# The eight column-tiled output matmuls of a state-space channel group, issued as one run led by the last state

## The chip, the cores and the metric

The kernel runs on one core of a Trainium2 chip. Its time is the device time of one execution in microseconds (us); of several executions the median is taken. The engines are named as in the profile: PE is TensorE (matmuls), PEld its weight loads, DVE is VectorE, ACT is ScalarE, POOL is GpSimd, SP is SyncE, which here only issues DMAs. Each engine works through its own queue in the order in which its instructions were put there.

## The reference, cut to what matters

One layer of a decoder trunk with 256 positions and 4096 channels, everything in float32. A normalised input is multiplied by one combined projection, whose columns feed three mixers (pooling, stick-breaking attention and a state-space mixer); the gated mixer outputs go through one output projection and a final norm. The change lies in the state-space mixer, of which this is the core:

```python
bu = jnp.einsum('blgc,gpc->blgp', ug.astype(jnp.complex64), b_bar)
a = jnp.broadcast_to(lam_bar, bu.shape)
...
_, states = lax.associative_scan(combine, (a, bu), axis=1)
y = jnp.einsum('blgp,gcp->blgc', states, c_mat).real.reshape(bsz, L, D_SSM)
y = y + d_skip.astype(jnp.float32) * uf
h = jax.nn.gelu(y)
```

There are 64 groups of 16 channels with 64 complex states each. The change concerns the second product: the real part of the states times the complex output matrix, that is, real part times real part minus imaginary times imaginary.

## The kernel before

**The main stream.** All large products are one stream of 528 weight blocks of 256 rows by 512 columns (the list `subs`; the projection, the gated linear unit of the state-space mixer, and the output projection one after the other). A block is loaded by SP (`load`, L175), split by ACT into a high part (`hi`, L120 through `hi_lo`, L210) and by DVE into the remainder (`lo`, L212), and then multiplied in `mm_tok`: for each half of the positions and each of the two row tiles three matmuls, high by high (L317), high by low (L324) and low by high (L325), into the PSUM tile `pm`. Loads run four blocks ahead and splits two blocks ahead of the matmuls; the split parts go round in a ring of four buffers. In the output stage some blocks go through `mm_seven` (L284) with seven products in place of eight.

**Side work.** The mixers are generators that yield after each small step. They wait in two queues, `side_q` and `ssm_q`; after each block `pump` takes some steps from them, for the state-space mixer 1.5 a block from block 30 on. This fixes the program order. What each engine does in which order is then planned by the framework from that order, the dependencies and a timeline simulation (`schedule_with_timeline_sim=True`, L1167); only SP's order is that of the program. A dependency of the kind NoSync that is added by hand with `tc.add_manual_dep` holds two instructions of the plan in order and adds no semaphore.

**The state-space mixer.** `ssm` works through eight channel groups `ct` of 128 channels, that is, eight of the reference's groups in each. For each group it makes `cf`, the output matrix with its scale, then four states `ss[0]` to `ss[3]`, each for two of the reference's groups (128 partitions, two components of 256 positions). Each state takes a PE product (`ps_bu`, L650), the rotation by tables (L658 to L662), two scans (L665), and the rotation back (L667, L668); component 0 is made at L670 and component 1, last of all, at L671. Four buffers (`s`) hold the states.

**The output matmuls.** When the fourth state is appended, L674 takes one of two PSUM banks shared by the small products (`ps`), and eight matmuls follow at L677: for each component `c` and each state `j`, the 128 rows of `cf[:, j, c, :]` with 32 columns as weights, the 256 positions of `ss[j][:, c, :]` as moving data, into the partitions 32j to 32j + 31 of `ps_y`. A matmul with 32 columns uses a quarter of the PE array, a column tile; the four values of `j` use four different ones. Component 0 starts the sum and component 1 closes it. Since the operands are float32, each such matmul is shown as two instructions in the trace. The matmuls of `c` = 0 need `ss[j][:, 0, :]` alone, so they may leave before the later states are there.

Behind them, DVE adds the skip term (`y`, L682, shown as L117) and reads `ps_y`; ACT and DVE make the GELU, and its product goes back into `uT(ct)` (L687), which the gated linear unit reads much later. The next group's `cf` and states may only overwrite the old ones when the eight matmuls are done.

Of the kernel before, what the change touches and what calls it, by code (L numbers as in the profile page):

```python
# [21 lines left out]
L = 256  # L22
# [55 lines left out]
def body(tc, a, out, ctx):  # L78
    nc = tc.nc
    V, S, T, G = nc.vector, nc.scalar, nc.tensor, nc.gpsimd  # L80
# [512 lines left out]
    def ssm(sp, wait_u):  # L593
# [11 lines left out]
        for ct in range(8):  # L605
# [5 lines left out]
            cf = sp.tile([P, 4, 2, 32], F32, tag="cf", bufs=1, name="cf")  # L611
# [6 lines left out]
            ss = []  # L618
            for half in range(2):
# [3 lines left out]
                for m in range(4, 8):  # L623
                    n = 1 << m
                    for j in range(2):
                        c, sn = (pw[:, m, x, 4 * ct + 2 * half + j:4 * ct + 2 * half + j + 1] for x in range(2))
# [19 lines left out]
                for j in range(2):  # L646
                    pr = 4 * ct + 2 * half + j
                    ps = pk.tile([P, 2, L], F32, tag="ps", bufs=2, name="ps_bu")
# [23 lines left out]
                    ss.append(s)  # L672
                    yield
            ps = pk.tile([P, 512], F32, tag="ps", bufs=2, name="ps_y")  # L674
            for c in range(2):
                for j in range(4):
                    T.matmul(ps[32 * j:32 * j + 32, 0:L], cf[:, j, c, :], ss[j][:, c, :], start=c == 0, stop=c == 1, skip_group_check=True)  # L677
            yield
            y = sp.tile([P, L], F32, tag="yg", bufs=1, name="y")
            z = sp.tile([P, L], F32, tag="zg", bufs=1, name="z")  # L680
# [139 lines left out]
    ep = op = None  # L820
    apool = None
    ssm_q.append(ssm(sp, lambda ct: ct < u_done[0]))
    glu_sums = cp.tile([P, 2, 2], F32, name="glu_sums")
    out_sums = cp.tile([P, 2, 4], F32, name="out_sums")
# [152 lines left out]
    for i, (ui, at, h, s) in enumerate(subs):  # L977
        kind, c, nk = units[ui]
# [8 lines left out]
        if at == 0 and h == 0:  # L987
# [4 lines left out]
            else:  # L992
                ps = [pm.tile([P, NU], F32, tag="c%d" % t, bufs=2, name="pm") for t in range(2)]
# [16 lines left out]
        if seven(i):  # L1010
            if h == 0:
# [4 lines left out]
                j = SEVENS[c].index(s)  # L1016
# [37 lines left out]
    for t in range(2):  # L1054
        for h, at, wide, dst in ((0, 0, NU, out_sums[:, t, 3:4]), (1, 0, half, sums[:, t, 0:1]), (1, half, half, sums[:, t, 1:2])):
# [9 lines left out]
            if h == 0:  # L1065
                ss = cp.tile([P, 1], F32, name="ss_out%d" % t)
# [111 lines left out]
```

## Time and profile before

| | |
|---|---|
| median of three runs | 1518.77 us (1517.45 to 1519.06) |
| the profiled execution, its own time | 1519.82 us |
| the profiled execution, its span (first to last instruction) | 1518.0 us |
| mean granted TensorE clock | 0.998 of full speed |
| instructions | 19823 |
| bytes read and written | 371.28 MB and 48.76 MB |
| instructions of line 677 on PE | 128, from 185.1 to 780.4 us |

A busy time in the profile is the sum over an engine's instructions where overlapping ones count once. Ends of matmuls are modelled, so a matmul's shown duration is longer than the distance between two starts; distances between starts show the rate. A row of the timeline merges neighbouring instructions of one line (the number behind x). A window's row gives, for each engine, the busy time and the number of instructions in it. The chain of work follows the end of the execution back from instruction to instruction, each to what released it or to the one before it on its engine. "issue" is time in which an engine waited for nothing that the profile shows.

### The profile page before, as it was taken

How to read it: one execution, taken by the hardware profiler on the slowest of the kernel's cores; microseconds unless marked ns; L12 is line 12 of the kernel's file. 1: busy time of each engine (PE TensorE's matmuls, PEld its weight loads, DVE VectorE, ACT ScalarE, POOL GpSimd, SP SyncE). 2: the span in 40 equal slices, each digit the busy share in tenths (PEclk: the TensorE clock that was granted, in tenths of full speed). 3: DMA queues.
4: the chain of work that ended last, by engine and by line, in shares of the span. 5: the costliest groups of instructions: out<-in, count | busy, mean ns of one | idle time of the engine just before them, and what ended most of it. 6: DMA issues, size and time to landing. Idle time of an engine off the chain costs nothing.

```text
span 1518.0 us, 19823 instructions
## 1 busy us (share of the span) xinstructions
PE 1501.9 (99%) x6848; PEld 1232.7 (81%) x6848; DVE 1223.9 (81%) x1876; ACT 878.0 (58%) x1165; POOL 15.2 (1%) x31
## 2 busy tenths in 40 slices
PE   9999999999999999999999999999999999999996
PEld 7888888787878788888888888888888778888885
DVE  7479978898989898999875555576657898989897
ACT  7655455665655555545655544565546776757574
POOL 0000000000000000000000000000000000000000
PEclk9999999999999999999999999999999999999999
DMA  9766556576788886888678788689977989889895
GB/s 359 297 227 211 192 169 209 189 229 235 269 286 302 297 289 233 309 302 302 231 272 299 266 309 284 244 301 348 339 244 255 355 332 349 311 328 322 311 367 211
DMA packets 129508, 424.50 MB, mean 280 GB/s; under 512 B 15616, under 2 KB 21504, under 8 KB 129408
## 3 DMA queue, kind: packets, MB, share of 16 engines
q1 hardware_dynamic: 115504, 398.17, 74.1%
q0 software_dynamic: 3760, 14.16, 2.4%
q10 hardware_dynamic: 10144, 10.92, 2.4%
q8 instruction: 53, 0.87, 0.2%
q14 instruction: 47, 0.39, 0.1%
HBM read 371.28 MB, written 48.76 MB: 277 GB/s over the span
## 4 chain that ended last, share of the span: by engine, by line
PE 92%; DMA 3%; DVE 3%; issue 1%; ACT 0%; SPq 0%; DVEq 0%; ACTq 0%
PE pm L317 26%; PE pm L325 26%; PE pm L324 26%; PE p L284 6%; PE pm L284 5%; DMA w<-in_ws 2%; DVE lo L212 1%; PE ps_y L677 1%; PE ps_c L771 1%; PE ps_bu L650 1%; DMA yk<-kept 1%; PE ps_p L459 0%; PE ps_t L375 0%; PE ps_z L702 0%; DVE ts L108 0%
## 5 line engine op out<-in xcount | busy, mean ns | idle before, releaser
L212 DVE TENSOR_TENSOR lo<-w,hi 128x1024 fp32r<-128x1024 f32 (+1 forms) x531 | 619.7, 1174 | 233.2 <-ACT hi L120 231.6
L120 ACT ACTIVATE hi<-w 128x1024 fp32r<-128x1024 f32 (+1 forms) x531 | 539.1, 1020 | 461.8 <-PE pm L325 350.6
L324 PE MATMUL pm<-lo,xhl 128*128 128x512 f32 x1714 | 669.2, 391 | 0.7 <-DVE lo L212 0.7
L325 PE MATMUL pm<-hi,xhl 128*128 128x512 f32 x1714 | 669.0, 391 | 0.0
L317 PE MATMUL pm<-hi,xhl 128*128 128x512 f32 x1714 | 661.1, 391 | 1.2 <-ACT xhl L120 0.6
L317 PEld LDWEIGHTS pm<-hi,xhl 128*128 128x128 f32 x1714 | 322.2, 188 | 69.7 <-issue 2.1
L325 PEld LDWEIGHTS pm<-hi,xhl 128*128 128x128 f32 x1714 | 322.2, 188 | 68.2 <-issue 2.9
L324 PEld LDWEIGHTS pm<-lo,xhl 128*128 128x128 f32 x1714 | 322.4, 188 | 67.8 <-DVE lo L212 1.6
L120 ACT ACTIVATE hi<-t 128x1024 fp32r<-128x1024 f32 x84 | 86.2, 1052 | 38.0 <-DVE t L108 20.8
L212 DVE TENSOR_TENSOR lo<-t,hi 128x1024 fp32r<-128x1024 f32 x84 | 100.9, 1221 | 4.1 <-ACT hi L120 3.6
L284 PE MATMUL pm<-hi,xhl 128*128 128x512 f32 x168 | 65.5, 390 | 0.0
L284 PE MATMUL p<-hi,xhl 128*128 128x512 f32 x168 | 65.2, 391 | 0.0
L284 PE MATMUL p<-hi,y 128*128 128x512 f32 x168 | 64.1, 389 | 0.0
L117 DVE SCALAR_TENSOR_TENSOR et<-et,pw,tr 128x16 f32<-128x16 f32 (+3 forms) x256 | 55.8, 276 | 3.0 <-ACT tr L120 2.7
L120 ACT ACTIVATE tr<-et,pw 128x32 f32<-128x32 f32 (+3 forms) x128 | 44.9, 384 | 17.9 <-DVE et L117 8.3
L108 DVE TENSOR_TENSOR pre<-pre 128x512 f32<-128x512 f32 x68 | 46.7, 687 | 0.9
L665 DVE TENSOR_TENSOR_SCAN tb<-rho,ta 128x256 f32<-128x256 f32 x64 | 40.6, 676 | 0.2
L284 PEld LDWEIGHTS p<-hi,xhl 128*128 128x128 f32 x168 | 31.5, 188 | 7.4 <-ACT hi L120 1.0
L284 PEld LDWEIGHTS p<-hi,y 128*128 128x128 f32 x168 | 31.5, 188 | 6.5
L284 PEld LDWEIGHTS pm<-hi,xhl 128*128 128x128 f32 x168 | 31.5, 188 | 6.5
L284 PE MATMUL pm<-hi,y 128*128 128x512 f32 x84 | 32.8, 390 | 1.1 <-ACT hi L120 1.1
L284 PE MATMUL p<-lo,xhl 128*128 128x512 f32 x84 | 32.8, 391 | 0.1
(248 smaller groups left out, 1174.8 us busy)
## 6 DMA issues: line engine op xcount, KB each, us to landing
w<-in_ws SPq DMA_DIRECT2D x493, 512.0 KB, 4.9
pre<-in_ws SPq DMA_DIRECT2D x68, 512.0 KB, 7.0
sums<-pre SPq DMA_DIRECT2D x68, 512.0 KB, 5.5
t<-sums SPq DMA_DIRECT2D x68, 512.0 KB, 7.4
w<-in_ws SPq DMA_DIRECT2D x36, 256.0 KB, 6.9
xsq<-in_xr SPq DMA_DIRECT2D x8, 512.0 KB, 6.5
o<-in_xr SPq DMA_DIRECT2D x8, 512.0 KB, 8.3
xt<-in_xT SPq DMA_DIRECT2D x15, 256.0 KB, 6.1
```

The lines of the kernel that those rows point to most:

```text
L108: V.tensor_tensor(o, x, y, op)
L117: V.scalar_tensor_tensor(o, x, s, y, op0, op1)
L120: return S.activation(o, x, f, **kw)
L212: state["split"] = V.tensor_tensor(dst_lo, src, dst_hi.bitcast(F32), ALU.subtract).ins.name
L284: T.matmul(o, stat[:, p, :], pair[q][:, n], start=start and k == 0, stop=stop and k == 2, skip_group_check=True)
L317: made = T.matmul(o, stat[:, slot, 0, sl], hi[:, n], start=begin, stop=False, skip_group_check=True)
L324: T.matmul(o, stat[:, slot, 0, sl], lo[:, n], start=False, stop=False, skip_group_check=True)
L325: made = T.matmul(o, stat[:, slot, 1, sl], hi[:, n], start=False, stop=end, skip_group_check=True)
L650: T.matmul(ps[:, c, :], b3r[:, j, c, :], u3r[:, j, :], start=c == 0, stop=True, skip_group_check=True)
L665: V.tensor_tensor_scan(tb[:, c, :], rho[:, pr:pr + 1].broadcast_to([P, L]), ta[:, c, :], 0.0, ALU.mult, ALU.add)
L677: T.matmul(ps[32 * j:32 * j + 32, 0:L], cf[:, j, c, :], ss[j][:, c, :], start=c == 0, stop=c == 1, skip_group_check=True)
L771: T.transpose(ps[:, (c * 2 + t) * P:(c * 2 + t + 1) * P], z[:, t, (h * 2 + c) * P:(h * 2 + c + 1) * P], ident)
```

## The change

The order of the eight matmuls is turned round: component 1 comes first and now starts the sum, component 0 closes it; within a component the state order is 3, 0, 1, 2. The first matmul therefore reads component 1 of state 3. Each of the other seven is given a NoSync dependency on this first one, so that none of them can stand ahead of it in PE's order. Operands, sizes and the number of instructions stay as they are.

```diff
             ps = pk.tile([P, 512], F32, tag="ps", bufs=2, name="ps_y")
-            for c in range(2):
-                for j in range(4):
-                    T.matmul(ps[32 * j:32 * j + 32, 0:L], cf[:, j, c, :], ss[j][:, c, :], start=c == 0, stop=c == 1, skip_group_check=True)
+            first = None
+            for c in (1, 0):
+                for j in (3, 0, 1, 2):
+                    made = T.matmul(ps[32 * j:32 * j + 32, 0:L], cf[:, j, c, :], ss[j][:, c, :], start=c == 1, stop=c == 0, skip_group_check=True)
+                    if first is None:
+                        first = made.ins.name
+                    else:
+                        tc.add_manual_dep(
+                            made.ins, first,
+                            mybir.DependencyInfo(mybir.DependencyClass.NoSync, mybir.DependencyReason.DATA),
+                            reason="all in one run",
+                        )
             yield
```

## The prediction

> **What bounds the kernel now.** I read the page's engine totals first, then the chain that ended last, then the waits of TensorE. From the page:
>
> ```profile
> PE 1501.9 (99%) x6848; PEld 1232.7 (81%) x6848; DVE 1223.9 (81%) x1876; ACT 878.0 (58%) x1165; POOL 15.2 (1%) x31
> ...
> PE 92%; DMA 3%; DVE 3%; issue 1%; ACT 0%; SPq 0%; DVEq 0%; ACTq 0%
> PE pm L317 26%; PE pm L325 26%; PE pm L324 26%; PE p L284 6%; PE pm L284 5%; DMA w<-in_ws 2%; DVE lo L212 1%; PE ps_y L677 1%; PE ps_c L771 1%; PE ps_bu L650 1%; DMA yk<-kept 1%; PE ps_p L459 0%; PE ps_t L375 0%; PE ps_z L702 0%; DVE ts L108 0%
> ```
>
> TensorE (PE) is busy for 99% of the span and carries 92% of the chain. Matmuls of the weight stream (L317, L324, L325) make up most of it, and the matmuls of this change (ps_y, L677) stand on the same chain with about 1%. So the question is how much PE time the eight output products take, and how much of that is the price of being issued in pieces.
>
> A busy PE can hide slow issue, so I measure in starts. The PE timeline around channel group 0 (start, length of the merged row, line, count):
>
> ```profile
> 182.75 0.39 PE L325 MATMUL pm<-hi,xhl 128*128 128x512 f32 x1
> ...
> 184.79 0.39 PE L325 MATMUL pm<-hi,xhl 128*128 128x512 f32 x1
> 185.11 0.63 PE L677 MATMUL ps_y<-s,cf 128*32 128x256 f32 x6
> 185.68 0.50 PE L317 MATMUL pm<-hi,xhl 128*128 128x512 f32 x1
> 186.01 0.39 PE L324 MATMUL pm<-lo,xhl 128*128 128x512 f32 x1
> ...
> 187.63 0.39 PE L325 MATMUL pm<-hi,xhl 128*128 128x512 f32 x1
> 187.95 1.05 PE L677 MATMUL ps_y<-s,cf 128*32 128x256 f32 x10
> 188.93 0.50 PE L317 MATMUL pm<-hi,xhl 128*128 128x512 f32 x1
> 189.26 0.39 PE L324 MATMUL pm<-lo,xhl 128*128 128x512 f32 x1
> ```
>
> The first two rows are nine stream matmuls apart: (184.79 - 182.75) / 9 = 0.227 us a start. Around the ps_y run of six, two stream starts that would be 0.454 us apart (184.79 to the second stream matmul after the run, 186.01) are 1.22 us apart: the run costs 0.77 us. The run of ten costs 187.63 to 189.26 less 0.454, 1.18 us. Each column matmul shows as two instructions, so these are three matmuls (states 0, 1, 2 of component 0) and five (the rest).
>
> Two groups are cut three times, as the timeline around group 2 shows:
>
> ```profile
> 336.41 0.39 PE L317 MATMUL pm<-hi,xhl 128*128 128x512 f32 x1
> 336.73 0.62 PE L677 MATMUL ps_y<-s,cf 128*32 128x256 f32 x4
> 337.29 0.50 PE L324 MATMUL pm<-lo,xhl 128*128 128x512 f32 x1
> 337.62 0.39 PE L325 MATMUL pm<-hi,xhl 128*128 128x512 f32 x1
> ```
>
> ```profile
> 343.55 0.39 PE L324 MATMUL pm<-lo,xhl 128*128 128x512 f32 x1
> 343.87 0.62 PE L677 MATMUL ps_y<-s,cf 128*32 128x256 f32 x2
> 344.42 0.50 PE L325 MATMUL pm<-hi,xhl 128*128 128x512 f32 x1
> 344.75 0.39 PE L317 MATMUL pm<-hi,xhl 128*128 128x512 f32 x1
> ```
>
> In the same way the run of four costs 1.21 - 0.454 = 0.76 us and the run of two 1.20 - 0.454 = 0.75 us. What is to be seen: two, four or six instructions last 0.62 to 0.63 us and cost the same, 0.75 to 0.77 us. Products that go to different column tiles lie beside each other; only the two instructions of one tile follow each other. The run of ten is longer because column tile 3 has two matmuls in it, four instructions deep: (1.05 - 0.62) / 2 = 0.215 us a level. So a run's price is a fixed part for entering and leaving the narrow tiles, 0.75 - 2 x 0.215 = 0.32 us, plus 0.215 us for each level of its deepest tile.
>
> How many runs there are comes from the windows of line 677, one window for each group (PE busy, then the count):
>
> ```profile
> 180.00:190.00 10.00, 1.68 (x16) 0.53 (x16) 1.00 0.67 211
> ...
> 334.00:358.00 24.00, 2.29 (x16) 0.66 (x16) 1.00 0.67 217
> ...
> sum 139.00, PE 14.69 PEld 4.48; mean PE 1.84 PEld 0.56
> ```
>
> 1.68 is one run of 0.63 and one of 1.05; 2.29 is two of 0.62 and one of 1.05. The sum 14.69 over eight windows is six of the first kind and two of the second (6 x 1.68 + 2 x 2.29 = 14.66). So today there are 6 x 2 + 2 x 3 = 18 runs.
>
> **The change part by part.** *Removed:* ten of the 18 runs. *Added:* six instructions (in the two groups with three runs, three matmuls from two places) to the last run of each group, which then holds all 16. The tile order 3, 0, 1, 2 repeated twice puts four instructions on every column tile, so the deepest tile stays at four levels: 0.32 + 4 x 0.215 = 1.18 us, and I add 0.02 us for the wider lower levels: 1.20 us. No trace shows 16 in one run. The bounds: not below the 1.18 us of the run of ten, which is as deep; at most six more levels in single file, 1.18 + 6 x 0.215 = 2.47 us. I take 1.20 because runs of two, four and six already differ by 0.02 at most.
>
> Saved in a two-run group: 0.77 + 1.18 - 1.20 = 0.75 us; in a three-run group 0.76 + 0.75 + 1.18 - 1.20 = 1.49 us. Sum: 6 x 0.75 + 2 x 1.49 = **7.5 us**. At the upper bound it would be 6 x (1.95 - 2.47) + 2 x (2.69 - 2.47) = -2.7 us, a loss.
>
> One rule of the Trainium skill speaks against the packed figure. The window of 0.2 us at the head of the run of ten shows, for this line, PE and then weight loads (PEld):
>
> ```profile
> 187.90:188.10 0.20, 0.15 (x4) 0.15 (x8) 1.00 1.10 328
> ```
>
> Eight weight loads start within 0.15 us while four matmuls are in flight, so loads for narrow tiles lie beside matmuls and beside each other. The page "TensorE: Matmul & The Clock Gate", section Part 3: Packing small matmuls — row/col tiling, says that a weight load overlaps with matmuls in flight only where the row group differs; all column tiles here use the same 128 rows, so by it none would. Here the trace speaks against it.
>
> *Moved:* the whole product now waits for the state made last, component 1 of state 3, which leads. Today the first run leaves before that. An added wait on PE holds up everything behind it, here the stream matmuls, and behind them ScalarE, which waits for PE to free the split buffers, and VectorE's y. What does the wait cost? From the VectorE timeline for groups 0 and 5 (s is the state, both components merged), and from the PE timeline for group 5:
>
> ```profile
> 183.66 0.75 DVE L108 TENSOR_TENSOR s<-ta,tb 128x256 f32<-128x256 f32 x2
> ...
> 603.08 0.76 DVE L108 TENSOR_TENSOR s<-ta,tb 128x256 f32<-128x256 f32 x2
> ```
>
> ```profile
> 607.15 1.05 PE L677 MATMUL ps_y<-s,cf 128*32 128x256 f32 x10
> ```
>
> State 3 is complete at 184.41 and 603.84; the run of ten starts at 187.95 (above) and 607.15. So both components lie ready 3.5 and 3.3 us before the run leaves. Component 1 is made one VectorE step (about 0.4 us) after component 0, which released that run in the plan; the new lead moves later by about that, and the margin stays. I take nothing for the wait, covered by these 3 us. Without the cover each microsecond of standing costs 8 us over the groups. Below nothing it cannot go: the run cannot leave before the state is there.
>
> The run of ten also tells whether all 16 will stay together: there, too, one matmul is released by the newest state and four that were ready follow it, and it stands uncut in the groups quoted and, by the windows (one more cut would add a run of 0.62), in all eight. No DMA is issued or moved, and no VectorE or ScalarE instruction is added. The first matmul of each accumulation now is component 1 instead of 0; that costs nothing.
>
> **Does the end follow?** PE time saved between 185 and 781 us reaches the end only if nothing else limits the later work:
>
> ```profile
> 450.00:800.00 350.00, 350.00 (x1649) 286.65 (x1648) 312.33 (x530) 189.76 (x263) 1.07 (x2) 1.00 0.82 283
> 1300.00:1400.00 100.00, 100.00 (x442) 82.79 (x442) 92.83 (x100) 68.56 (x79) 0.68 (x1) 1.00 0.89 320
> ```
>
> PE has no idle time in either stretch; VectorE is next, at 312.33 / 350 = 89% and 93%. Shortening the first stretch by about 1% takes VectorE to about 90%: it becomes tighter, not the bound. From the table of waits:
>
> ```profile
> ACT hi L120 <- PE pm L325: 355.3, 266, 2.9
> ```
>
> The splitting of weights, and with it VectorE and the loads, waits for PE for 355.3 us in total. These move forward with PE, so I carry the whole 7.5 us to the end. The profiled execution took 1519.82 us, its span 1518.0; it would become 1512.3 with a span of 1510.5. The median of the runs before is 1518.77, 1.05 below the profiled execution, so I predict a median of 1518.77 - 7.5 = **1511.3 us**.
>
> **The rivals.** *Part of the gain given back by a new plan.* The instruction order is planned over the whole program, so a change at 185 us can move splits, loads and side work after it. The table of PE's waits has these of the stream's own (line, what it waited for: total, times, longest):
>
> ```profile
> PE pm L284 <- ACT hi L120: 1.1, 1, 1.1
> PE pm L317 <- DVE gl L108: 0.7, 1, 0.7
> PE pm L324 <- DVE lo L212: 0.7, 1, 0.7
> PE pm L317 <- ACT xhl L120: 0.6, 1, 0.6
> PE pm L317 <- DVE ss_out L1067: 0.5, 1, 0.5
> ```
>
> These are 3.6 us. If a new order brings as many again, the time is 1511.3 + 3.6 = 1514.9. VectorE's 93% in the output stage speaks for it; that the table has only one more, ahead of the first matmuls of all, speaks against it.
>
> *Swallowed in the output stage.* The chain that ended last leaves PE in that stage (start, length):
>
> ```profile
> 1428.29 0.24 PE pm L325
> ...
> 1428.56 0.97 ACT hi L120
> ...
> 1431.95 6.71 DMA w<-in_ws
> ```
>
> If loads and VectorE bound that stage by themselves, the saved time would turn into stalls there: 1518.8. Against it: the chain enters this piece from a split (ACT hi, 1428.56) that starts as a matmul ends, so the piece moves with PE.
>
> *The run does not stay whole.* If the planner sends the lead alone and the other 14 later, each group has a run of two (0.75) and one of 14 (at most 1.20): nothing saved in six groups, 2 x 0.74 = 1.5 us in two: 1517.3. Against it stands the uncut run of ten.
>
> *Weight loads between the levels.* Levels three and four hold one load each today and four then. If three more loads of 0.109 us had to stand in each, that is 2 x 3 x 0.109 = 0.65 us a group, 5.2 us: 1516.5.
>
> ```profile
> L677 PEld LDWEIGHTS ps_y<-s,cf x128: 106/109/110, 185.1 to 780.2; 128*32 128x32 f32 x128
> ```
>
> That is how the rule of that page of the Trainium skill would come out. The eight loads in 0.15 us speak against it.
>
> *Slower: PE stands at the lead.* The waits of VectorE for this product today (total, times, longest):
>
> ```profile
> DVE y L117 <- PE ps_y L677: 6.6, 7, 1.8
> ```
>
> Once the lead is at the head of PE's queue, the stream behind it cannot pass. It decides from 7.5 / 8 = 0.94 us of standing a group. The plan's clock and the chip's differ: VectorE today waits up to 1.8 us for ps_y, PE today has 3.3 us to spare. Were this turned round and PE waited 1.8 us in every group, 8 x 1.8 = 14.4 us would be added: 1511.3 + 14.4 = 1525.7. For it: only the planner's clock keeps the margin. Against it: the margin is above 3 us in the groups read, and the lead moves later by only one VectorE step.
>
> **How the numbers follow.** Forecast 0.66; part given back 0.14; swallowed 0.06; not whole 0.04; weight loads 0.03; slower 0.07 (in it 0.02 for a run in single file, 1518.8 + 2.7 = 1521.5). A measurement of this kernel tells about 0.2%, 3.0 us, from no change: faster is below 1515.7. Of the part given back I count 0.09 as faster and 0.05 as the same. Faster: 0.66 + 0.09 = 0.75; same: 0.05 + 0.06 + 0.04 + 0.03 = 0.18; slower 0.07. The range goes from 1508.8 (a new plan that also removes 2.5 of the 3.6 us of stalls) to 1517.0, which leaves out the swallowed, the cut and the slower cases, 0.17.
>
> **What would show it.** Right: eight ps_y runs of 16, each lasting about 1.07 us and costing about 1.20 us between stream matmuls; line 677's weight loads idle before them eight times, not 18; no PE wait on a state. Wrong: runs cut by stream matmuls; a run above 1.3 us; an idle PE ahead of ps_y released by VectorE; or new PE stalls after 800 us that add up to the missing time.

## The result, and the profile after

The changed kernel takes **1510.47 us** (median of four, 1510.05 to 1511.52) against 1518.91 us of the kernel before (median of four, the three above and one more): a ratio of 0.9945, 95% interval 0.9932 to 0.9957, 8.4 us less. The forecast was 1511.3 us. The profiled execution took 1510.62 us with a span of 1508.8 us; before it was 1518.0 us.

From the page of the changed kernel, engine totals and the chain that ended last:

```profile
PE 1492.9 (99%) x6848; PEld 1232.6 (82%) x6848; DVE 1222.3 (81%) x1876; ACT 878.5 (58%) x1165; POOL 15.2 (1%) x31
...
PE 94%; DMA 2%; DVE 2%; issue 1%; ACT 0%; SPq 0%; DVEq 0%; ACTq 0%
```

PE's busy time fell by 9.0 us with the same 6848 matmuls, and the span by 9.2; the other engines did the same work as before. The bound is the same, PE at 99%, with less to do. Line 677 is now line 678. Its windows, one for each channel group as before (PE busy, count; weight loads, count), the first and the last of eight:

```profile
180.00:190.00 10.00, 1.07 (x16) 0.42 (x16) 1.00 0.67 197
...
765.00:782.00 17.00, 1.07 (x16) 0.42 (x16) 1.00 0.89 308
sum 149.00, PE 8.56 PEld 3.34; mean PE 1.07 PEld 0.42
```

The sum 8.56 is eight times 1.07: each product is one run, where before the eight windows held 14.69. What such a run costs is read from the PE timeline of group 0:

```profile
188.44 0.39 PE L325 MATMUL pm<-hi,xhl 128*128 128x512 f32 x1
188.76 1.07 PE L678 MATMUL ps_y<-s,cf 128*32 128x256 f32 x16
189.76 0.50 PE L317 MATMUL pm<-hi,xhl 128*128 128x512 f32 x1
190.10 0.40 PE L324 MATMUL pm<-lo,xhl 128*128 128x512 f32 x1
```

The stream starts around it lie 190.10 - 188.44 = 1.66 us apart; less two undisturbed steps of 0.227 us the run costs 1.21 us. Sixteen instructions cost 0.03 us more than the ten of before (1.18). This is the only run of the eight that stands alone. Six others have a pair of `ps_bu` matmuls directly behind them, and the last has four of `ps_c` beside it. In group 2 the run and its pair cost 1.45 us together (359.24 - 357.34 - 0.454); the 20 pairs that stand alone cost 0.25 us each on average, so 1.20 us is left for the run.

The wait that the change adds, in group 5, which had the smallest margin of the groups read before (VectorE, then PE timeline):

```profile
599.45 0.76 DVE L108 TENSOR_TENSOR s<-ta,tb 128x256 f32<-128x256 f32 x2
```

```profile
603.09 1.07 PE L678 MATMUL ps_y<-s,cf 128*32 128x256 f32 x16
```

State 3 is complete at 600.21 and the run leaves at 603.09: 2.9 us of cover are left of 3.3. Read in the same way in all eight groups, the cover is 2.9 to 4.5 us; ahead of the last run of each group before it was 3.3 to 5.0 us. The table of PE's waits has no row for ps_y at all:

```profile
PE ps_i L137 <- DVE zeros L134: 1.2, 1, 1.2
PE pm L317 <- ACT hi L120: 1.2, 1, 1.2
PE pm L317 <- ACT xhl L120: 0.9, 1, 0.9
PE pm L317 <- DVE gl L108: 0.7, 1, 0.7
PE pm L317 <- DVE ss_out L1076: 0.5, 1, 0.5
PE pm L284 <- ACT hi L120: 0.3, 1, 0.3
PE pm L324 <- DVE lo L212: 0.2, 1, 0.2
```

Behind the first row, which lies ahead of the stream, these are 3.8 us; before they were 3.6. So the saving was not paid back in new stalls. The line's weight loads, too, idle before them eight times, where before it was 18 times, once for each run.

### The profile page after: what moved, and what is told of

Its sections match the earlier page's. It is cut to its first block, busy times and chain, and to the rows that moved or that the text cites. A ratio compares the mean times of both kernels' runs of the same rounds, so it can differ in the third digit from the quotient of the medians.

```text
span 1508.8 us, 19821 instructions
## 1 busy us (share of the span) xinstructions
PE 1492.9 (99%) x6848; PEld 1232.6 (82%) x6848; DVE 1222.3 (81%) x1876; ACT 878.5 (58%) x1165; POOL 15.2 (1%) x31
## 4 chain that ended last, share of the span: by engine, by line
PE 94%; DMA 2%; DVE 2%; issue 1%; ACT 0%; SPq 0%; DVEq 0%; ACTq 0%
PE pm L317 26%; PE pm L325 26%; PE pm L324 26%; PE p L284 7%; PE pm L284 5%; DMA w<-in_ws 2%; DVE lo L212 1%; PE ps_c L780 1%; PE ps_bu L650 1%; PE ps_y L678 1%; PE ps_p L459 0%; PE ps_z L711 0%; PE ps_t L375 0%; DVE ts L108 0%; DMA prm<-in_prm 0%
## 5 line engine op out<-in xcount | busy, mean ns | idle before, releaser
L324 PE MATMUL pm<-lo,xhl 128*128 128x512 f32 x1714 | 668.4, 390 | 0.2 <-DVE lo L212 0.2
L317 PE MATMUL pm<-hi,xhl 128*128 128x512 f32 x1714 | 660.5, 391 | 2.6 <-ACT hi L120 1.2
L317 PEld LDWEIGHTS pm<-hi,xhl 128*128 128x128 f32 x1714 | 322.1, 188 | 69.5 <-ACT xhl L120 1.8
L284 PE MATMUL pm<-lo,xhl 128*128 128x512 f32 x84 | 32.7, 389 | 0.0
```

What stands on the lines that cost most here:

```text
L284: T.matmul(o, stat[:, p, :], pair[q][:, n], start=start and k == 0, stop=stop and k == 2, skip_group_check=True)
L317: made = T.matmul(o, stat[:, slot, 0, sl], hi[:, n], start=begin, stop=False, skip_group_check=True)
L324: T.matmul(o, stat[:, slot, 0, sl], lo[:, n], start=False, stop=False, skip_group_check=True)
```

## The experiments

### The order without the dependencies

The order of the change is kept and the added dependencies are dropped.

```diff
-                    if first is None:
-                        first = made.ins.name
-                    else:
-                        tc.add_manual_dep(
...
-                            reason="all in one run",
-                        )
```

Expected:

> The changed order of the eight matmuls without the added dependencies. Theory (the lead by the state made last holds the run together, the dependency adds nothing): eight runs of 16 instructions, 1510.5 us. Rival (the dependency holds the run together): 18 runs as before, 1518.9 us.

Measured: 1509.78 us, ratio to before 0.9945 (0.9928 to 0.9961). The windows of line 678 sum to the same as with the dependencies:

```profile
sum 149.00, PE 8.56 PEld 3.34; mean PE 1.07 PEld 0.42
```

Eight whole runs, so the dependencies add nothing; on every engine the instructions stand in the same order as in the changed kernel. What holds the seven others back is the plan itself. In all the kernels here the lengths of the runs fit a plan that keeps the eight matmuls in the order of the program. The kernel before shows it too: at 185.11 six instructions left, those of component 0 of states 0 to 2, though component 1 of these states lay ready as well; in the kernel that goes state by state, below, twelve leave at that place. So whichever matmul stands first in the program holds back the other seven. That the planner does this because all eight write one PSUM tile is likely, but no run tests it.

### Component 1 first, led by the state made first

The kernel before, with only the components exchanged.

```diff
-            for c in range(2):
+            for c in (1, 0):
                 for j in range(4):
-                    T.matmul(..., start=c == 0, stop=c == 1, skip_group_check=True)
+                    T.matmul(..., start=c == 1, stop=c == 0, skip_group_check=True)
```

Expected:

> The kernel before with component 1 first and the states in their old order 0, 1, 2, 3, without dependencies: the lead is the state made first. Theory (only a lead by the state made last keeps the run whole): 18 runs as before, 1518.9 us. Rival (turning the components round is what brings the gain): 1510.5 us.

Measured: 1518.45 us, ratio 1.0001 (0.9992 to 1.0011). The windows of line 677 in this kernel, the first and the last of eight:

```profile
180.00:190.00 10.00, 1.68 (x16) 0.53 (x16) 1.00 0.72 209
...
765.00:782.00 17.00, 1.68 (x16) 0.53 (x16) 1.00 0.79 276
sum 152.00, PE 14.69 PEld 4.49; mean PE 1.84 PEld 0.56
```

The busy sum is that of the kernel before, and so is the time. Turning the components round brings nothing by itself.

### Component 0 first, led by the state made last

The changed kernel, with the components put back.

```diff
-            for c in (1, 0):
+            for c in (0, 1):
                 for j in (3, 0, 1, 2):
-                    made = T.matmul(..., start=c == 1, stop=c == 0, skip_group_check=True)
+                    made = T.matmul(..., start=c == 0, stop=c == 1, skip_group_check=True)
```

Expected:

> The changed kernel with component 0 first again, still led by state 3 and with the dependencies. The lead is one VectorE step older than in the changed kernel. The planned order differs in some places from the changed kernel's. Theory (the lead by the last state is all that matters, and the wait for its second component is covered): eight runs of 16, PE never idle ahead of them, 1510.5 us, within 2 us. Rival (the wait for component 1 costs or gains something, or the new plan and not the runs brought the gain): more than 2 us away from 1510.5.

Measured: 1510.47 us, ratio 0.9949 (0.9936 to 0.9961). Again eight whole runs:

```profile
sum 149.00, PE 8.57 PEld 3.34; mean PE 1.07 PEld 0.42
```

Which component of state 3 leads makes no difference that can be measured. With the run before this separates the parts of the change: the lead by the last state carries all of it. It also speaks against a lucky plan: this kernel's order differs from the changed kernel's in places on PE, VectorE and ScalarE, and its time is the same.

### Both matmuls of a tile next to each other

The changed kernel, with the loops exchanged; the run stays whole, the order inside is 3, 3, 0, 0, 1, 1, 2, 2.

```diff
-            for c in (1, 0):
-                for j in (3, 0, 1, 2):
+            for j in (3, 0, 1, 2):
+                for c in (1, 0):
```

Expected:

> The changed kernel with the two loops exchanged, so that the two matmuls of a column tile stand next to each other (3, 3, 0, 0, 1, 1, 2, 2); the run stays whole. Theory A (a run lasts as long as its deepest column tile, whatever the order inside): a run costs 1.20 us as in the changed kernel, 1510.5 us. Theory B (matmuls start strictly in the order of the queue, so a tile waits until the second matmul of the tile before it has started): the four tiles follow one another, three of them add two to three levels of 0.215 us each, 1.3 to 1.9 us a run, 10 to 16 us in all: 1521 to 1526 us.

Measured: 1510.24 us, ratio 0.9949 (0.9934 to 0.9964). The PE timeline has the run of group 0:

```profile
187.76 1.09 PE L678 MATMUL ps_y<-s,cf 128*32 128x256 f32 x16
```

It is 0.02 us longer, not 1.3 to 1.9. The window of 0.2 us at its head holds these instructions of the line on PE:

```profile
187.75:187.95 0.20, 0.19 (x4) 1.00 1.06 318
```

Four instructions are in flight within 0.2 us, less than the 0.215 us of one level, although the program's first four instructions (two matmuls) all belong to tile 3. So tiles do not queue behind one another: theory A, the depth of the deepest tile, holds, and theory B falls. The page "TensorE: Matmul & The Clock Gate" of the Trainium skill says in its section Part 3: Packing small matmuls — row/col tiling that matmuls start and end strictly in program order; with the program's order here that would have been theory B. Whether PE starts them out of order or the two instructions of each matmul are already put in another order in the queue, the trace, which knows starts, does not tell.

### State by state, in the order in which the states are made

The kernel before, with the loops exchanged. This cuts the product more often.

```diff
-            for c in range(2):
-                for j in range(4):
+            for j in range(4):
+                for c in (0, 1):
```

Expected:

> The kernel before with the two loops exchanged, so that both matmuls of a state stand together and the states follow in the order in which they are made. In the planned order the product is then cut into 22 runs in place of 18: eight of one matmul, six of two, two of four, six of six. Theory (0.32 us for a run and 0.215 us for each level of its deepest tile, all of it on the path): 8 x 0.75 + 6 x 1.18 + 2 x 1.18 + 6 x 1.20 = 22.6 us against 17.1 us before: 1518.9 + 5.5 = 1524.4 us. Rival (the price of the cuts is hidden, and the gain came from the new plan): within 2 us of 1518.9.

Measured: 1524.20 us, ratio 1.0040 (1.0025 to 1.0055), 5.9 us above the 1518.28 us of the kernel before beside it. The PE timeline of group 0, whose product is now cut into three:

```profile
185.21 0.39 PE L325 MATMUL pm<-hi,xhl 128*128 128x512 f32 x1
185.53 1.08 PE L677 MATMUL ps_y<-s,cf 128*32 128x256 f32 x12
186.54 0.50 PE L317 MATMUL pm<-hi,xhl 128*128 128x512 f32 x1
186.88 0.40 PE L324 MATMUL pm<-lo,xhl 128*128 128x512 f32 x1
...
187.59 0.40 PE L324 MATMUL pm<-lo,xhl 128*128 128x512 f32 x1
187.91 0.62 PE L677 MATMUL ps_y<-s,cf 128*32 128x256 f32 x2
188.46 0.51 PE L325 MATMUL pm<-hi,xhl 128*128 128x512 f32 x1
188.90 0.62 PE L677 MATMUL ps_y<-s,cf 128*32 128x256 f32 x2
189.45 0.50 PE L317 MATMUL pm<-hi,xhl 128*128 128x512 f32 x1
189.78 0.39 PE L324 MATMUL pm<-lo,xhl 128*128 128x512 f32 x1
```

Twelve instructions on three tiles, four levels deep, last 1.08 us and cost 186.88 - 185.21 - 0.454 = 1.22 us. Two instructions on one tile still cost what a run costs: from 187.59 to 189.78 there are two of them and three stream steps, (2.19 - 0.68) / 2 = 0.75 us each. The busy times of the line's windows, about 2.31 us in four groups, 2.13 in two and 3.17 in two, fit the 22 runs that were expected (three, two and three in a group). The law of a fixed part and 0.215 us a level gave 5.5 us more; 5.9 came. The price of a cut is on the path in this direction too, and the rival, a price that is hidden, falls.

### The stream held behind the run

The changed kernel, with the slower rival's condition made true: in the program's next block the stream matmul of L317 depends on the run's last matmul, so PE has to stand until the state is there.

```diff
+            state["y_mm"] = made.ins.name
             yield
...
+                if "y_mm" in state:
+                    tc.add_manual_dep(
+                        made.ins, state.pop("y_mm"),
+                        mybir.DependencyInfo(mybir.DependencyClass.NoSync, mybir.DependencyReason.DATA),
+                        reason="the stream behind the run",
+                    )
                 if "held" in state:
```

Expected:

> The changed kernel with one more order held by hand: the first stream matmul that follows a run in the program may not stand ahead of that run in PE's order. The planned order puts the later runs up to 350 rows of PE's order further ahead, so the margin between the state and the run is gone. The output is the same. Theory (a PE that stands at the lead is paid for one to one, as the slower rival says): PE's waits ahead of ps_y appear in the trace, 20 to 80 us in all, and the time is 1510.5 us plus that sum. Rival (PE's standing is made up later): PE waits, but the time stays within 5 us of 1510.5.

Measured: 1569.95 us, ratio 1.0340 (1.0324 to 1.0356), 59.5 us above the changed kernel. PE's waits (total, times, longest), the first four rows:

```profile
PE ps_y L684 <- DVE et L628: 31.3, 5, 8.5
PE ps_y L684 <- DVE s L108: 6.0, 1, 6.0
PE ps_z L736 <- ACT ah L120: 4.3, 2, 3.0
PE ps_av L747 <- ACT aw L120: 1.8, 2, 0.9
```

PE now stands ahead of six of the eight runs, 37.3 us in all. The first row names `et`, a small copy that VectorE starts as the state's last step ends; in all six cases the state is complete 0.14 us before the run leaves, so it is the state that PE waits for. One to one would give 1510.5 + 37.3 = 1547.8 us; 22 us more came. Where they come from shows in the PE timeline behind a stand:

```profile
271.44 1.93 PE L684 MATMUL ps_y<-s,cf 128*32 128x256 f32 x16 [7.24 <-DVE et L628]
273.31 0.80 PE L317 MATMUL pm<-hi,xhl 128*128 128x512 f32 x1
273.90 0.63 PE L330 MATMUL pm<-lo,xhl 128*128 128x512 f32 x1
274.33 0.63 PE L331 MATMUL pm<-hi,xhl 128*128 128x512 f32 x1
```

After 7.24 us of standing the run lasts 1.93 us where it lasted 1.07, and the stream steps 0.43 us apart where it stepped 0.227. The windows there show why (time, PE, weight loads, VectorE, ScalarE and POOL, then the granted clock):

```profile
264.00:266.00 2.00, 0.20 (x2) 0.00 (x0) 1.73 (x3) 1.15 (x2) 0.00 (x0) 1.00 0.35 139
266.00:268.00 2.00, 0.00 (x0) 0.00 (x0) 1.90 (x5) 0.00 (x0) 0.00 (x0) 0.87 0.06 16
268.00:270.00 2.00, 0.00 (x0) 0.00 (x0) 1.93 (x4) 0.00 (x0) 0.00 (x0) 0.50 0.18 49
...
278.00:280.00 2.00, 2.00 (x10) 1.66 (x9) 1.44 (x3) 1.60 (x4) 0.00 (x0) 1.00 0.20 45
```

The granted clock falls to 0.50 while PE stands and is back at 1.00 in the window from 278. So the mechanism of the slower rival is real, and the one-to-one price was too low: a stand also takes half the clock from the microseconds behind it.

The two traces also show how the 22 us divide. The stream's matmuls can be matched one for one in any two traces. Between the two that start at 180.03 and 800.10 us in the kernel before, this kernel's stream falls 63.1 us behind that of the changed kernel. PE stands for 44.5 us of this: the 37.3 us ahead of the runs and 7.2 us elsewhere, nearly all of it in the attention, where the changed kernel has no such waits. For another 35.0 us PE works at a granted clock of 0.50; with a stream step of 0.43 us in place of 0.227 that is an estimated 16.5 us. Together these are 61.0 of the 63.1 us. Outside that stretch this kernel is 3.6 us faster than the changed one, so at most that much is made up.

## Why the prediction was right

**The count of runs** (18 to 8) came out exactly. The reason given, that the uncut run of ten shows what a lead by the newest state does, was right, and the experiments narrow it: the lead alone does it, the dependencies and the turned components do nothing.

**The price of a run.** The step of the sum was 1.20 us for 16 instructions; 1.21 us was measured. By the prediction's own costs the 18 runs before took 17.1 us, and now eight take 8 x 1.21 = 9.7 us: 7.4 us less, against 7.5 in the sum. The upper bound, single file, was far off, and so was the rival of the weight loads, which asked for 0.65 us more in a run. The prediction put the fixed 0.32 us down to the narrow tiles without a comparison. The trace of the kernel before has one, eight float32 instructions of the same 256 columns at full width (`ps_p`, L459). The chain of work has them as one piece:

```profile
152.92 1.73 PE ps_p L459 x8
```

The stream starts around them are 152.53 and 154.71, so they cost 2.18 - 0.454 = 1.73 us: 0.216 us for each and nothing on top. So the fixed part does come with the narrow tiles.

**The added wait.** The cover was to stay; 2.9 us of 3.3 stayed in group 5, and PE never waited for the lead. The held stream shows that this was a condition and not a matter of course. That the first run leaves before state 3 is there is true of seven groups. In group 0 it left at 185.11, 0.7 us after the state was complete (184.41), and the run of ten followed only at 187.95. There the cut was made by the plan alone, and not by a missing operand.

**What reaches the end.** The whole saving did, as PE's unchanged stalls (3.8 us against 3.6) and the three kernels with whole runs (ratios 0.9945 to 0.9949) show. The rivals of a swallowed gain, of a gain given back and of a run that does not stay whole fell.

**What is left over.** The medians lie 8.4 us apart and the two profiled spans 9.2, more than the 7.5 us of the sum. Where the difference arises shows when the stream's matmuls, 6204 in every kernel, are matched one for one. The stream matmul that starts at 180.03 us in the kernel before starts at 180.28 in the changed kernel, and the one at 800.10 starts at 792.36: between the two 7.99 us are gained. The same for the other kernels, each in one execution (us gained on the kernel before):

| kernel | runs | up to 180 us | 180 to 800 us | 800 to 1150 us | after 1150 us | whole span |
|---|---|---|---|---|---|---|
| changed | 8 | -0.25 | 7.99 | -0.09 | 1.56 | 9.21 |
| without the dependencies | 8 | 0.15 | 7.99 | -0.38 | 1.96 | 9.72 |
| component 0 first | 8 | 0.75 | 7.99 | -0.32 | -0.06 | 8.35 |
| tile by tile | 8 | 0.76 | 7.83 | -0.07 | 0.16 | 8.67 |
| component 1 first | 18 | 0.54 | -0.28 | -0.05 | 1.24 | 1.45 |
| state by state | 22 | -0.42 | -5.90 | -0.04 | 1.78 | -4.58 |

In the stretch of the state-space mixer the gain follows the runs: about 8 us with eight, about nothing with 18, a loss of 5.9 with 22. Of the 7.99 us, 7.53 are the price of small products between stream matmuls, measured as in the prediction over all of them (84.21 us before, 76.68 after). The other 0.46 lies in the next nine or so stream steps behind such an interruption, which take up to 0.232 us in place of 0.227; the prediction left them out. What comes up to 180 us and after 1150 us does not follow the runs. The kernel with component 1 first, which has all 18, gains 1.2 us after 1150 us as well; and the changed kernel and the one that goes tile by tile, whose plans differ only inside the runs, lie 1.4 us apart there. So the rest of the 9.2 us is scatter between executions, from 1516.89 to 1521.16 us in 13 of the kernel before.

## What to carry to other kernels

Where PE is the bound and small matmuls on column tiles interrupt a stream of full-width ones, count the runs, not the matmuls: here a run cost 0.32 us for going in and out and 0.215 us for each level of its deepest tile, in any order and with the other tiles free. To keep such a group whole, let the matmul whose operand comes last stand first in the program; in all the kernels here with such a lead the others, which write the same PSUM tile, left with it. Before doing so, read from the trace how long the last operand lies ready before the run, because a PE that has to stand for it pays the wait, and a slower clock behind it.

## What the runs showed that was not expected

The order of the two loops inside a run is almost free: with both matmuls of a tile next to each other the run took 1.09 us against 1.07, and the eight runs together cost 0.16 us (7.99 - 7.83 in the table above).

Standing is dearer than its length. In the kernel with the held stream even a short stand, ahead of group 6's run, took the clock down; timeline, then windows:

```profile
670.39 1.94 PE L684 MATMUL ps_y<-s,cf 128*32 128x256 f32 x16 [2.09 <-DVE et L628]
```

```profile
669.50:670.00 0.50, 0.00 (x0) 0.00 (x0) 0.50 (x2) 0.00 (x0) 0.00 (x0) 1.00 1.05 418
670.00:670.50 0.50, 0.11 (x4) 0.14 (x8) 0.50 (x3) 0.00 (x0) 0.00 (x0) 0.75 1.08 442
670.50:671.00 0.50, 0.50 (x8) 0.30 (x11) 0.50 (x2) 0.00 (x0) 0.00 (x0) 0.50 0.97 393
```

After 2.09 us of idling the granted clock went from 1.00 to 0.50 just as the run began, and the run lasted 1.94 us. PE had also stood for 0.47 us shortly before, up to 666.87. In the attention of the same kernel the clock fell to 0.50 by 585 us, after stands of only 1.29, 0.66 and 0.90 us with a few matmuls between them. The page "TensorE: Matmul & The Clock Gate" of the Trainium skill, section Part 1: The HAM clock gate (the "warmup" mystery), gives at least one idle window of about 3.4 us before the clock is halved; in this run an idle time shorter than that was enough.
